# Attention's reciprocal sums: from two TensorE transposes to a store and two broadcast loads

## The chip, the cores and the metric

The kernel runs on one core of a Trainium2 chip. A core has five engines, each with its own queue of instructions, worked off in order: TensorE (PE, matrix products, transposes among them), VectorE (DVE), ScalarE (ACT), GpSimd (POOL) and SyncE (SP, which here only issues DMAs). Engines wait for each other through semaphores. A DMA is issued by an instruction on the queue of SP, ACT or POOL, and whatever stands behind that instruction waits with it. TensorE writes into PSUM, eight banks of 2 KB per partition; GpSimd works on SBUF here. The metric is the device time of one execution in microseconds (us), as the median of several runs.

## The reference, cut to what matters

The program is two layers of a diffusion trunk (a convolution layer, then an attention layer, each with a SwiGLU FFN) over 1024 latent tokens and 256 context tokens. The change touches the attention of the second layer: 16 heads of 64 channels, which share 4 key/value heads, 1280 keys.

```python
def gqa_sdpa(q, k, v):
    B, Q, H, Dh = q.shape
    qg = q.reshape(B, Q, N_KV_HEADS, KV_GROUP, Dh)
    s = jnp.einsum("bqkgd,bskd->bkgqs", qg, k).astype(jnp.float32) * (Dh ** -0.5)
    p = jax.nn.softmax(s, axis=-1).astype(v.dtype)
    o = jnp.einsum("bkgqs,bskd->bqkgd", p, v)
    return o.reshape(B, Q, H * Dh)
```

The kernel leaves the division of the softmax to the end: it multiplies the values with the bare exponentials and scales the result by the reciprocal of their sum. That last step is what is changed.

## The kernel before

Attention works in **units**. A unit is one key/value head `t` (with its four query heads) and one block `qt` of 128 queries; there are 4 x 8 = 32. Units run in two streams of 16: first the queries 0 to 511, then 512 to 1023. In each unit:

- `load_q` (L1102) fetches the queries from DRAM by a DMA on GpSimd's queue, into one of two slots. Unit n+2 uses the slot of unit n, so its load waits until TensorE has read that one.
- `scores` (L1116 to L1124): for each of the four heads, TensorE computes 128 x 1280 scores into one of two places in PSUM; VectorE scales them and takes the row minimum (L1122); ScalarE takes the exponential and sums it along the row (L1124). The sums of the four heads stand in `sums[:, 0, :]`, with the query as the partition.
- `values` (L1128 to L1158) goes over ten blocks `j` of 128 keys. TensorE transposes the four heads' exponentials (L1134); ScalarE rounds them into a high part (L1137) and VectorE takes the rest (L1138); TensorE multiplies both with the values (L1140, L1141) into the one PSUM bank of the kind `av`. The two halves of a value row (high and low part) come out on the two halves of the partitions, with the channel as the partition and the query along the row.
- the end of `values`: VectorE takes the reciprocal of the sums (L1145). GpSimd copies each of the four reciprocals 64 times along the row (L1147). ScalarE copies one half of the bank to `tmp` (L1151) and VectorE adds the other (L1152), for each half of the partitions. Two TensorE transposes (L1155) turn the copied reciprocals, so that the query runs along the row, into the same bank `av`, and VectorE multiplies (L1156). `done` stores the result in DRAM (`od`, L1450, GpSimd's queue), except for the last unit of a stream, whose result stays in SBUF as `olast`.

`values` of a unit and `scores` of the next are woven into one another (`attn_stream`), and a scheduler then sets each engine's order by priorities; the products with the values are put later by `lav`. So TensorE finishes a unit's values at about the time when it has finished the scores of the second unit after it.

What stands around it: the first units of stream one run beside the last query projections (`qkv`), the others of that stream **alone**. At the end of stream one comes the **hand-over**: `out_proj` loads `od` back (L1485), splits it into a high and a low part (L161 on ScalarE, L164 on VectorE), the last unit's from `olast`, and projects it. The second stream runs in the background of that, of the norm behind it (L761, L763) and of the FFN for the first half of the queries; `pump` gives it a share of each step. At its **end** the second `out_proj` does the same, with `T1` as its input, `T2` and `T5` as the two split parts. `T1`, `T5` and `HS` hold the exponentials before that.

Of the kernel before, what the change touches and what calls it, by code (L numbers as in the profile page):

```python
# [8 lines left out]
F32 = mybir.dt.float32  # L9
# [3 lines left out]
ALU = mybir.AluOpType  # L13
AX = mybir.AxisListType

P = 128
# [4 lines left out]
TOK = CTX + SEQ  # L21
# [3 lines left out]
NH, NKV, HD = 16, 4, 64  # L25
# [30 lines left out]
class Kern:  # L56
# [1071 lines left out]
    def values(self, t, Ps, sums, dst, done):  # L1128
        nc, c = self.nc, self.c
        av = self.bank("av")  # L1130
        for j in range(NJ):
            tp = self.bank("pt")
            for h in range(4):
                nc.tensor.transpose(tp[:, h * P:(h + 1) * P], Ps[h][:, j * P:(j + 1) * P], c["ident"])  # L1134
            ph, pl = self.ptring[self.ptslot % len(self.ptring)]
            self.ptslot += 1
            nc.scalar.copy(ph, tp)  # L1137
            nc.vector.tensor_tensor(pl, tp, ph.bitcast(F32), op=ALU.subtract)  # L1138
            with self.later(self.lav):
                nc.tensor.matmul(av, lhsT=self.value(t, j), rhs=ph, start=j == 0, stop=False)  # L1140
                nc.tensor.matmul(av, lhsT=self.value(t, j), rhs=pl, start=False, stop=j == NJ - 1)  # L1141
            yield 0.87

        r = sums[:, 1, :]
        nc.vector.reciprocal(r, sums[:, 0, :])  # L1145
        rx = self.sb(256)
        nc.gpsimd.tensor_copy(rx.rearrange("p (h d) -> p h d", d=HD), r.unsqueeze(2).to_broadcast([P, 4, HD]))  # L1147
        tmp = self.sb(256).rearrange("p (a q) -> p a q", q=P)
        v = av.rearrange("p (a b q) -> p a b q", b=2, q=P)
        for b, r, o in ((0, slice(0, 64), slice(64, 128)), (1, slice(64, 128), slice(0, 64))):  # L1150
            nc.scalar.copy(tmp[r], v[o, :, b, :])  # L1151
            nc.vector.tensor_tensor(dst[r], v[r, :, b, :], tmp[r], op=ALU.add)  # L1152
        rb = self.bank("av")
        for a in range(2):
            nc.tensor.transpose(rb[:, a * P:(a + 1) * P], rx[:, a * P:(a + 1) * P], c["ident"])  # L1155
        nc.vector.tensor_tensor(dst, dst, rb[:, 0:256].rearrange("p (a q) -> p a q", q=P), op=ALU.mult)  # L1156
        done()
        yield 0.1  # L1158

# [270 lines left out]
    def attention(self, final, qr):  # L1430
        nc, a, c = self.nc, self.a, self.c
        kbuf = self.T("T3", [P, 2 * TOK], F32R)
        pr1 = self.T("T1", [P, 3, TOK])
        prh = self.T("HS", [P, 4, TOK])
        ptt = self.T("T2", [P, 4, 2, 512], F32R)
        self.ptring = [(ptt[:, i, 0], ptt[:, i, 1]) for i in range(4)]
# [6 lines left out]
        def dst(q0):  # L1443
            def of(t, q):
                if (t, q % 4) == (NKV - 1, 3):
                    return self.olast, lambda: None
                st = self.sb(256).rearrange("p (a q) -> p a q", q=P)

                def done():
                    nc.gpsimd.dma_start(self.od[:, 2 * t:2 * t + 2, q * P:(q + 1) * P], st)  # L1450
                return st, done
            return of
# [11 lines left out]
        pr4 = None  # L1464
        for us in self.attn_stream(units, (self.kub, kbuf), dst(0), True):
            if self.bgq:
                self.pump(self.rate * us)
            elif pr4 is None:
                pr4 = self.T("T5", [P, 3, TOK])
                self.pring = self.pring[:4] + [pr4[:, 0], pr4[:, 1], pr4[:, 2]] + self.pring[4:]  # L1470
                self.set_banks(**alone)
                self.sring = [0, TOK]
# [78 lines left out]
        yacc, n = self.acc(CTX), CTX  # L1551
# [172 lines left out]
```

## Time and profile before

| | |
|---|---|
| median of 3 runs | 2939.41 us (2938.95 to 2943.35) |
| the profiled execution | 2938.98 us, its span 2937.2 us |
| TensorE clock granted, mean | 0.987 |
| attention units | first reciprocal at 1605.2 us, last at 2362.6 us |

How to read it. The span runs from the first instruction to the last. A row of a group of instructions names the line, the engine, the operation, what it writes and reads (tiles by name, `ps` is PSUM, `T` any of the large tiles `T1` to `T6`, `cst` the constants with the identity), shapes, how often, then the busy time in us and the mean of one in ns, then the idle time of the engine just before them and who ended it. PEld is TensorE's loading of weights, which runs beside its products. A chain of work is followed back from the last instruction of a window: at each step to what released it. Where a chain is all PE, other engines had nothing to do with the length of that stretch.

### The profile page before, as it was taken

How to read it: one execution, taken by the hardware profiler on the slowest of the kernel's cores; microseconds unless marked ns; L12 is line 12 of the kernel's file. 1: busy time of each engine (PE TensorE's matmuls, PEld its weight loads, DVE VectorE, ACT ScalarE, POOL GpSimd, SP SyncE). 2: the span in 40 equal slices, each digit the busy share in tenths (PEclk: the TensorE clock that was granted, in tenths of full speed). 3: DMA queues.
4: the chain of work that ended last, by engine and by line, in shares of the span. 5: the costliest groups of instructions: out<-in, count | busy, mean ns of one | idle time of the engine just before them, and what ended most of it. 6: DMA issues, size and time to landing. Idle time of an engine off the chain costs nothing.

```text
span 2937.2 us, 42731 instructions
## 1 busy us (share of the span) xinstructions
PE 2847.7 (97%) x16462; PEld 2446.1 (83%) x16462; DVE 2160.7 (74%) x3746; ACT 1335.5 (45%) x2229; POOL 222.6 (8%) x377
## 2 busy tenths in 40 slices
PE   7999989999999999999999999989999999999998
PEld 6888877888888889989888787767777778889997
DVE  6887788847556378877786899786666666786777
ACT  5222255532222245544445688645555543444444
POOL 0000001011022001000011111110000000010000
PEclk9999999999999999999999999999999999999999
DMA  6443444334356224333345211322222143353332
GB/s 249 140 120 98 116 131 145 135 116 143 115 175 198 65 74 165 114 104 112 109 156 170 88 46 46 97 87 81 66 73 83 60 149 99 110 170 104 102 98 75
DMA packets 131755, 336.58 MB, mean 115 GB/s; under 512 B 31328, under 2 KB 52864, under 8 KB 130656
## 3 DMA queue, kind: packets, MB, share of 16 engines
q1 hardware_dynamic: 78016, 222.33, 24.1%
q0 software_dynamic: 29344, 103.83, 10.7%
q10 hardware_dynamic: 24192, 7.70, 1.1%
q8 instruction: 129, 2.11, 0.3%
q14 instruction: 74, 0.61, 0.1%
HBM read 289.50 MB, written 38.93 MB: 112 GB/s over the span
## 4 chain that ended last, share of the span: by engine, by line
PE 86%; DVE 7%; ACT 2%; issue 2%; DMA 2%; ACTq 0%; POOL 0%; SPq 0%; DVEq 0%; POOLq 0%
PE ps L172 15%; PE ps L173 15%; PE ps L174 15%; PE ps L875 4%; PE ps L877 4%; PE ps L876 4%; PE ps L1116 4%; PE ps L1134 4%; PE ps L1140 2%; PE ps L454 2%; PE ps L455 2%; PE ps L456 2%; PE ps L1141 2%; PE ps L185 1%; PE ps L183 1%
## 5 line engine op out<-in xcount | busy, mean ns | idle before, releaser
L172 PE MATMUL ps<-T,wh 128*128 128x512 f32 (+1 forms) x1360 | 502.5, 370 | 1.4 <-ACT T L161 0.8
L174 PE MATMUL ps<-T,wl 128*128 128x512 f32 (+1 forms) x1360 | 500.4, 368 | 2.0 <-DVE wl L148 2.0
L173 PE MATMUL ps<-T,wh 128*128 128x512 f32 (+1 forms) x1312 | 481.4, 367 | 0.2 <-DVE T L164 0.2
L144 ACT CAST wh<-wr 128x1024 fp32r<-128x1024 f32 (+1 forms) x217 | 225.0, 1037 | 419.9 <-PE ps L173 307.2
L148 DVE TENSOR_TENSOR wl<-wr,wh 128x1024 fp32r<-128x1024 f32 (+1 forms) x217 | 261.9, 1207 | 168.5 <-ACT wh L144 167.1
L875 PE MATMUL ps<-T,wh 128*128 128x256 f32 x1092 | 310.7, 285 | 5.0 <-ACT wh L161 4.5
L876 PE MATMUL ps<-T,wh 128*128 128x256 f32 x1092 | 306.5, 281 | 0.0
L877 PE MATMUL ps<-T,wl 128*128 128x256 f32 x1092 | 305.4, 281 | 0.2 <-DVE wl L164 0.2
L1138 DVE TENSOR_TENSOR T<-ps,T 128x512 fp32r<-128x512 f32 x320 | 216.8, 687 | 107.6 <-ACT T L1137 106.8
L172 PEld LDWEIGHTS ps<-T,wh 128*128 128x128 f32 x1360 | 257.8, 190 | 43.7 <-ACT T L1506 1.7
L174 PEld LDWEIGHTS ps<-T,wl 128*128 128x128 f32 x1360 | 257.7, 190 | 42.4 <-DVE wl L148 2.2
L173 PEld LDWEIGHTS ps<-T,wh 128*128 128x128 f32 x1312 | 248.5, 189 | 38.2 <-DVE T L164 1.3
L1137 ACT CAST T<-ps 128x512 fp32r<-128x512 f32 x320 | 186.0, 586 | 191.1 <-PE ps L1134 177.6
L173 PE MATMUL ps<-HS,wh 128*128 128x512 f32 x656 | 257.9, 393 | 0.0
L172 PE MATMUL ps<-HS,wh 128*128 128x512 f32 x608 | 238.4, 392 | 0.9 <-ACT wh L144 0.9
L174 PE MATMUL ps<-HS,wl 128*128 128x512 f32 x608 | 237.5, 391 | 0.0
L875 PEld LDWEIGHTS ps<-T,wh 128*128 128x128 f32 x1092 | 206.1, 189 | 11.2 <-ACT wh L161 6.7
L876 PEld LDWEIGHTS ps<-T,wh 128*128 128x128 f32 x1092 | 206.6, 189 | 0.5
L877 PEld LDWEIGHTS ps<-T,wl 128*128 128x128 f32 x1092 | 206.2, 189 | 0.6 <-DVE wl L164 0.4
L1134 PE MATMUL ps<-cst,T 128*128 128x128 f32 x1100 | 189.6, 275 | 3.2 <-DVE T L1138 3.1
L1122 DVE TENSOR_SCALAR_CACHE_REDUCE T<-ps,rq 128x1280 f32<-128x1280 f32 x110 | 170.0, 1546 | 27.9 <-PE ps L1116 22.1
L1134 PEld LDWEIGHTS ps<-cst,T 128*128 128x128 f32 x1100 | 132.6, 141 | 49.5 <-DVE T L1138 30.8
(377 smaller groups left out, 6195.9 us busy)
## 6 DMA issues: line engine op xcount, KB each, us to landing
wr<-in_w SPq DMA_DIRECT2D x170, 512.0 KB, 3.6
wr<-in_pw SPq DMA_DIRECT2D x35, 512.0 KB, 3.5
HV<-in_wmodT POOLq DMA_DIRECT2D x56, 256.0 KB, 4.1
q<-in_wmodT POOLq DMA_DIRECT2D x56, 256.0 KB, 3.9
KB<-in_w SPq DMA_DIRECT2D x24, 512.0 KB, 3.6
HR<-in_w SPq DMA_DIRECT2D x23, 512.0 KB, 3.7
q<-in_w SPq DMA_DIRECT2D x23, 512.0 KB, 4.2
q<-qsd POOLq DMA_DIRECT2D x32, 256.0 KB, 3.3
```

What stands on the lines that cost most here:

```text
L144: nc.scalar.copy(hi, raw)
L148: nc.vector.tensor_tensor(lo, raw, hi.bitcast(F32), op=ALU.subtract)
L172: nc.tensor.matmul(out[:, :n], lhsT=wh, rhs=xh, start=k == 0, stop=False)
L173: nc.tensor.matmul(out[:, :n], lhsT=wh, rhs=xl, start=False, stop=False)
L174: nc.tensor.matmul(out[:, :n], lhsT=wl, rhs=xh, start=False, stop=k == nk - 1)
L875: nc.tensor.matmul(out, lhsT=wh, rhs=bh, start=first and k == 0, stop=False, **skip)
L876: nc.tensor.matmul(out, lhsT=wh, rhs=bl, start=False, stop=False, **skip)
L877: nc.tensor.matmul(out, lhsT=wl, rhs=bh, start=False, stop=k == 3, **skip)
L1122: nc.vector.tensor_scalar(out=pt, in0=sc, scalar1=rq[:, h:h + 1], scalar2=None, op0=ALU.mult, op1=ALU.min, accum_out=mn)
L1134: nc.tensor.transpose(tp[:, h * P:(h + 1) * P], Ps[h][:, j * P:(j + 1) * P], c["ident"])
L1137: nc.scalar.copy(ph, tp)
L1138: nc.vector.tensor_tensor(pl, tp, ph.bitcast(F32), op=ALU.subtract)
```

## The change

The reciprocal is taken at the start of `values`, and the transposes, the copies for them and VectorE's multiply are gone. In their place three DMAs on GpSimd's queue: the 128 x 4 reciprocals go to DRAM turned (`rsd`, four rows of 128 numbers, stored as 512 pieces of four bytes), and two loads bring them back into `rb`, each row repeated over 64 partitions. GpSimd then multiplies the sum of the halves by `rb`. The copies and adds of the two halves stay as they are. There are two places for `rb`, at the ends of `T1` and `T5`, used in turn (only that in `T1` until `T5` is free). `rsd` has a place of its own for each unit.

```diff
     def values(self, t, Ps, sums, dst, done):
         nc, c = self.nc, self.c
         av = self.bank("av")
+        r = sums[:, 1, :]
+        nc.vector.reciprocal(r, sums[:, 0, :])
+        rd = self.rsd[self.unit]
+        rb = self.rbs[self.unit % len(self.rbs)]
+        self.unit += 1
+        nc.gpsimd.dma_start(rd.rearrange("h q -> q h"), r)
+        rv = rd.rearrange("(a b) q -> b a q", b=2)
+        for b in range(2):
+            nc.gpsimd.dma_start(rb[b * HD:(b + 1) * HD], rv[b:b + 1].to_broadcast([HD, 2, P]))
         for j in range(NJ):
...
-        r = sums[:, 1, :]
-        nc.vector.reciprocal(r, sums[:, 0, :])
-        rx = self.sb(256)
-        nc.gpsimd.tensor_copy(rx.rearrange("p (h d) -> p h d", d=HD), r.unsqueeze(2).to_broadcast([P, 4, HD]))
         tmp = self.sb(256).rearrange("p (a q) -> p a q", q=P)
         v = av.rearrange("p (a b q) -> p a b q", b=2, q=P)
         for b, r, o in ((0, slice(0, 64), slice(64, 128)), (1, slice(64, 128), slice(0, 64))):
             nc.scalar.copy(tmp[r], v[o, :, b, :])
             nc.vector.tensor_tensor(dst[r], v[r, :, b, :], tmp[r], op=ALU.add)
-        rb = self.bank("av")
-        for a in range(2):
-            nc.tensor.transpose(rb[:, a * P:(a + 1) * P], rx[:, a * P:(a + 1) * P], c["ident"])
-        nc.vector.tensor_tensor(dst, dst, rb[:, 0:256].rearrange("p (a q) -> p a q", q=P), op=ALU.mult)
+        nc.gpsimd.tensor_tensor(dst, dst, rb, op=ALU.mult)
         done()
         yield 0.1
@@ attention
-        pr1 = self.T("T1", [P, 3, TOK])
+        def place(tag):
+            t = self.T(tag, [P, 3 * TOK + 2 * P])
+            return t[:, :3 * TOK].rearrange("p (i n) -> p i n", i=3), t[:, 3 * TOK:].rearrange("p (a q) -> p a q", q=P)
+        pr1, rb = place("T1")
+        self.rbs, self.unit = [rb], 0
+        self.rsd = self.dp.tile([2 * NKV * 4, 4, P], F32, tag="rsd", name="rsd")
...
-                pr4 = self.T("T5", [P, 3, TOK])
+                pr4, rb = place("T5")
+                self.rbs.append(rb)
```

The scheduler's order moves with it. The lines of the changed kernel are 1143 for L1134, 1149 and 1150 for L1140 and L1141, 1147 for L1138, 1157 for L1152, 1457 for L1450, 1493 for L1485 and 1508 for L1500. Three places.

TensorE while attention runs alone, around the end of a head's scores (L1116); `T_13569` and `HS` hold exponentials, `T_13571` and `T_13572` the split ones, `HV` and `HR` values. Before:

```order
L1116 MATMUL ps<-KB,q 128x512
L1116 MATMUL ps<-KB,q 128x256 x2
L1116 MATMUL ps<-KB,q 128x512
L1155 MATMUL ps<-cst,sb 128x128 x2
L1116 MATMUL ps<-KB,q 128x512 x2
L1134 MATMUL ps<-cst,HS 128x128
L1134 MATMUL ps<-cst,T_13569 128x128
L1134 MATMUL ps<-cst,HS 128x128
L1134 MATMUL ps<-cst,T_13569 128x128
L1140 MATMUL ps<-T_13571,HV 128x512
L1141 MATMUL ps<-T_13571,HV 128x512
L1140 MATMUL ps<-T_13571,HV 128x512
```

The changed kernel (`T_14072` holds exponentials too):

```order
L1116 MATMUL ps<-KB,q 128x512 x4
L1116 MATMUL ps<-KB,q 128x256 x2
L1116 MATMUL ps<-KB,q 128x512 x4
L1143 MATMUL ps<-cst,T_13569 128x128
L1143 MATMUL ps<-cst,T_14072 128x128 x3
L1143 MATMUL ps<-cst,T_13569 128x128
L1143 MATMUL ps<-cst,T_14072 128x128 x3
L1116 MATMUL ps<-KB,q 128x256 x2
L1116 MATMUL ps<-KB,q 128x512
L1149 MATMUL ps<-T_13572,HV 128x512
L1150 MATMUL ps<-T_13572,HV 128x512
L1149 MATMUL ps<-T_13572,HV 128x512
```

The pair L1155 is gone, and ten scores and eight transposes stand in one piece each where before they were cut up differently from unit to unit; this piece comes again in every unit of the alone stage, and before only in the last one and the first.

GpSimd at the hand-over, from the last `q` load before it to the loads of `x2d`. Before:

```order
L1102 DMA q<-qsd 128x4x128
L1450 DMA od<-sb 128x2x128
L1485 DMA HS<-od 128x2x512 x3
L1147 COPY sb<-sums 128x256
L1450 DMA od<-sb 128x2x128
L1485 DMA HS<-od 128x2x384
L1500 DMA HS<-x2d 128x2x512 x3
```

The changed kernel, where L1136 stores the reciprocals, L1139 loads them back and L1158 multiplies:

```order
L1102 DMA q<-qsd 128x4x128
L1158 TENSOR_TENSOR sb<-sb,T_14072 128x256
L1457 DMA od<-sb 128x2x128
L1136 DMA rsd<-sums 128x4x1
L1139 DMA T_14072<-rsd 64x2x128 x2
L1493 DMA HS<-od 128x2x512 x3
L1158 TENSOR_TENSOR sb<-sb,T_13569 128x256
L1457 DMA od<-sb 128x2x128
L1493 DMA HS<-od 128x2x384
L1508 DMA HS<-x2d 128x2x512 x2
L1158 TENSOR_TENSOR olast<-olast,T_14072 128x256
```

The last unit's store of reciprocals and its loads now stand ahead of the loads of `od`, and the multiply of the unit before it between those. In a unit of the alone stage the order is the same without the loads of `od`: store, two loads, `q` load, multiply, `od` store.

VectorE at the end of the second stream, where it splits the input of the second output projection (L164, with `T_19816` or `T_19785` as the tile that lies in `T5`). Before:

```order
L1152 TENSOR_TENSOR olast<-ps,sb 64x256
L164 TENSOR_TENSOR T_19816<-T_19810,T_19815 128x512 x2
L1152 TENSOR_TENSOR olast<-ps,sb 64x256
L164 TENSOR_TENSOR T_19816<-T_19810,T_19815 128x512
L1156 TENSOR_TENSOR olast<-olast,ps 128x256
L164 TENSOR_TENSOR T_19816<-T_19810,T_19815 128x512 x3
```

The changed kernel:

```order
L1157 TENSOR_TENSOR olast<-ps,sb 64x256
L164 TENSOR_TENSOR HS<-sm,HS 128x512
L1157 TENSOR_TENSOR olast<-ps,sb 64x256
L164 TENSOR_TENSOR T_19785<-T_19779,T_19784 128x512 x6
L164 TENSOR_TENSOR T_19785<-T_19779,T_19784 128x2x384
```

The splits stand behind the last add, and the first of them waits for GpSimd's last multiply, which reads `rb` out of `T5`.

## The prediction

> **What bounds the kernel now.** I read the page first, then the windows of the attention, then the chain of work in each of them.
>
> ```profile
> span 2937.2 us, 42731 instructions
> PE 2847.7 (97%) x16462; PEld 2446.1 (83%) x16462; DVE 2160.7 (74%) x3746; ACT 1335.5 (45%) x2229; POOL 222.6 (8%) x377
> ```
>
> TensorE (PE) is busy for 97% of the span. The change sits in attention alone, from 1573 to 2394 us, so the question is what ends last there. The windows give it by stage (us, then busy time of PE, weight loads, VectorE, ScalarE, GpSimd, each with its number of instructions, then clock and DMA).
>
> ```profile
> 1665.00:1840.00 175.00, 170.43 (x1027) 139.84 (x1025) 159.78 (x263) 142.67 (x240) 25.20 (x41) 1.00 0.19 50
> 1840.00:1880.00 40.00, 37.15 (x198) 28.86 (x198) 33.52 (x55) 29.96 (x51) 9.12 (x13) 1.00 0.42 135
> 1970.00:2365.00 395.00, 394.96 (x2029) 311.00 (x2028) 262.50 (x387) 217.36 (x338) 28.46 (x46) 1.00 0.26 76
> ```
>
> Three stages. From 1665 to 1840 attention runs **alone**: PE shows 97%, but VectorE 91%. From 1840 to 1880 is the **hand-over** to the first output projection, with PE idle 2.9 us. From 1970 to 2365 the second half of the queries runs **beside** the FFN and PE is never idle. The chain of work names the releasers (shares of the window by engine and line; L1155 is the pair of transposes that goes).
>
> ```profile
> by line: PE ps L1134 20.2%; PE ps L1116 18.0%; PE ps L1140 14.2%; PE ps L1141 13.2%; DVE T L1138 10.1%; issue 7.6%; DVE T L1122 4.4%; ACT T L1137 4.3%; DVE HS L1122 3.7%; DVE sb L1152 2.2%; PE ps L1155 1.4%; ACT sb L1151 0.5%; ACT T L1124 0
> by line: PE ps L174 17.4%; PE ps L173 17.4%; PE ps L172 17.4%; PE ps L1116 15.7%; PE ps L1134 15.0%; PE ps L1140 8.1%; PE ps L1141 7.8%; PE ps L1155 1.2%; issue 0.0%
> L1155 PE MATMUL ps<-cst,sb 128*128 128x128 f32 x28 | 5.7, 285 | 0.0
> ```
>
> Beside the FFN every step of the chain is PE, so what leaves PE is gained; alone, VectorE and ScalarE hold a quarter of it, so removing PE work need not be.
>
> **The change part by part.** There are 32 units (a key/value head times 128 queries). Each loses two PE transposes (L1155) and a VectorE multiply out of PSUM (L1156), and gets one GpSimd multiply, a store of the reciprocals and two broadcast loads. GpSimd's copy L1147 goes.
>
> *Beside the FFN.* L1155 is 1.2% of a 395 us chain, 4.7 us for the 28 matmuls (14 units), 0.34 us a unit. All of it goes. The multiply moves to an engine that waits most of the time, and VectorE has 132 us idle there, so nothing takes its place. **-4.7 us.** Below, the gain is at least the 0.22 us a unit that the pair costs alone, 3.1 us.
>
> *Alone.* The pieces of the chain (start, length, what) show how a unit runs; each starts with the last scores of a head (L1116).
>
> ```profile
> 1796.27 0.73 PE ps L1116 x3
> 1797.00 0.23 PE ps L1155 x2
> ...
> 1809.28 0.74 PE ps L1116 x3
> ...
> 1825.67 0.74 PE ps L1116 x3
> ...
> 1833.50 1.48 DVE T L1122 x2
> ...
> 1837.63 0.33 DVE sb L1152
> 1837.96 1.19 DVE T L1138 x2
> 1839.15 1.48 DVE T L1122 x2
> ...
> 1840.68 0.74 PE ps L1116 x3
> 1836.85 2.33 PE L1116 MATMUL ps<-T,q 128*128 128x512 f32 x10
> ```
>
> Before, two patterns alternate: 1796.27 to 1809.28 is 13.01 us, 1809.28 to 1825.67 is 16.39 us, so a unit takes 14.70 us. Only the last unit, 1825.67 to 1840.68, issues ten scores in one piece, as the last row (timeline) shows, and takes 15.01 us: VectorE is the chain from 1832.81 to 1840.55. The order of the changed kernel has those ten scores in every unit. So I price its unit from this one: 15.01, less 0.22 for L1155, less what L1156 is worth.
>
> ```profile
> 1841.11 0.69 DVE L1138 TENSOR_TENSOR T<-ps,T 128x512 fp32r<-128x512 f32 x1
> 1841.72 0.41 DVE L1156 TENSOR_TENSOR sb<-sb,ps 128x256 f32<-128x256 f32 x1
> 1842.05 1.55 DVE L1122 TENSOR_SCALAR_CACHE_REDUCE T<-ps,rq 128x1280 f32<-128x1280 f32 x1
> ```
>
> L1156 holds the next L1122 back by 0.33 us (1841.72 to 1842.05). The exp behind it queues on ScalarE behind casts, so I take half, 0.165. That gives 15.01 - 0.22 - 0.165 = 14.63, against 14.70: 0.07 us times 11 units, **-0.8 us**. If nothing of either is worth anything, it is +0.31 times 11 = +3.4; if both patterns stay and both savings count whole, -0.55 times 11 = -6.
>
> The added wait is on GpSimd's queue: store, two loads that wait for the store to land, the q load (L1102) for a later unit, the multiply, the store of the result. How long the store of 512 four-byte pieces takes, no row shows, so I bound it.
>
> ```profile
> q1 hardware_dynamic: 78016, 222.33, 24.1%
> q10 hardware_dynamic: 24192, 7.70, 1.1%
> od<-sb POOLq DMA_DIRECT2D x30, 128.0 KB, 2.6
> x1d<-KB POOLq DMA_DIRECT2D x8, 128.0 KB, 2.0
> T<-in_xT SPq DMA_DIRECT2D x4, 512.0 KB, 10.6
> L1102 POOL DMA_DIRECT2D q<-qsd x12 | 9.2, 770 | 79.2 <-PE ps L1116 74.1 <-PE ps L1134 5.1
> ```
>
> Each DMA engine gets 32 pieces. A packet of q10 takes 1.1% of 16 engines' 2937 us over 24192, 21 ns; one of q1, far larger, 145 ns. With the quickest store's 2.0 us as the fixed part, that is 2.7 to 6.6 us; I take 4, between od's 2.6 and that end, and keep the slowest landing of the page, 10.6, for a rival. The q load's row says that before it waited 74.1 us for PE in 12 issues. It cannot go before PE has read the slot, and this comes some 10 us after the reciprocal (scores end at 1841.4, the reciprocal is at 1845.27, a unit is 14.7); store, 4 us and two loads are over by about 7. After it, a whole unit is left until q is read. So it is hidden, and is so up to a landing of some 8 us even before that unit is counted. Ahead of the first multiply the build sets one GpSimd instruction that no row prices; it stands in the second unit, and the q load behind it is for a unit that starts 15 us later.
>
> The multiply is bounded by a one-input copy and by a blocked one (POOL rows of the timeline and of the groups):
>
> ```profile
> L1147 POOL COPY sb<-sums 128x256 f32<-128x256 f32 x14 | 6.6, 472 | 46.1 <-PE ps L1134 23.2 <-issue 18.5 <-DVE sums L1145 4.5
> 2133.91 1.36 POOL L1147 COPY sb<-sums 128x256 f32<-128x256 f32 x1
> 2133.81 1.22 DVE L148 TENSOR_TENSOR wl<-wr,wh 128x1024 fp32r<-128x1024 f32 x1
> ```
>
> It costs 0.40 (the copy without disturbance) to 1.36 us; I take 0.6, near the copy. Its reader is a store that nobody reads for long, so between the ends it costs nothing. [...] The one long copy started while VectorE ran L148, which reads two SBUF inputs. [...] In the attention alone no VectorE instruction reads two SBUF tensors, and beside the FFN VectorE is idle a third of the time. So the sum stays as it is.
>
> *Hand-over.* GpSimd, ScalarE and VectorE rows of the timeline, in order of time:
>
> ```profile
> 1845.27 0.18 DVE L1145 RECIPROCAL sums<-sums 128x4 f32<-128x4 f32 x1 [0.47 <-ACT T L1124]
> 1848.28 2.16 POOL L1485 DMA_DIRECT2D HS<-od  x3 [5.14 <-PE ps L1134]
> 1852.81 1.14 ACT L161 CAST T<-HS 128x512 fp32r<-128x512 f32 x2
> 1854.44 0.73 POOL L1450 DMA_DIRECT2D od<-sb  x1 [3.59 <-DVE sb L1156]
> 1860.72 0.83 ACT L161 CAST T<-HS 128x768 fp32r<-128x768 f32 x1 [2.05 <-DMA HS<-od]
> ```
>
> After, the last unit's store and its two loads stand ahead of the three od loads (L1485). They are issued at 1845.27 + 0.2 + 0.8 + landing + 1.1, so with 4 us at 1851.4, 3.1 us late. ScalarE's splits (L161) and the casts behind them move by as much, but ScalarE waited 2.05 us for the fourth od load, which stays at its time, because the multiply of the last but one unit is ready soon after its adds and saves L1156's time. **+1.0 us**, with bounds 0 (landing 2.7) and +3.7 (landing 6.6).
>
> *End.* GpSimd's last multiply reads the broadcast from T5, and the split of the second output projection writes T5.
>
> ```profile
> 2389.64 1.29 DVE L164 TENSOR_TENSOR T<-T,T 128x512 fp32r<-128x512 f32 x2 [0.25 <-ACT T L161]
> 2390.97 0.43 DVE L1152 TENSOR_TENSOR olast<-ps,sb 64x256 f32<-64x256 f32 x1
> 2393.00 0.50 PE L172 MATMUL ps<-T,wh 128*128 128x512 f32 x1 [0.82 <-ACT T L161]
> ```
>
> The first splits (L164), at 2389.64 before, now wait for L1152's end at about 2391 plus 0.6 of multiply and two semaphores: some 2 us late. PE waited 0.82 us at 2393.0 anyway and has other matmuls to do: **+0.7 us**, between 0 and +1.5.
>
> *The seven other units* (two at the start, three in the hand-over, two later): 0.22 to 0.34 us each, **-1.7 us**.
>
> The sum is -4.7 - 0.8 + 1.0 + 0.7 - 1.7 = -5.5 us. The profiled execution took 2938.98 us (span 2937.2); the three runs' median, 2939.41, is 0.43 above it. So 2933.5 there, and 2934 against the median, which is 0.18% less. About 0.2% (5.9 us, below 2933.5 or above 2945.3) can be told from no change, so this forecast lies at that edge.
>
> **The rivals.**
> A. *Both savings whole in the attention alone.* The unit gets 0.37 to 0.55 us shorter, not 0.07, and the hand-over costs nothing: -4.7 - 5 - 1.7 + 0.4 = -11, 2928. For it: VectorE is the chain's longest run there and loses 0.33 us a unit. Against: the one unit with the new order was the slowest of its stage.
> B. *The new order is worse.* The ten scores wait for VectorE whatever else goes: +3.4 alone, hand-over +2, 2939 to 2940, no change. For it: VectorE's run of 7.74 us in that unit has neither L1155 nor L1156 in it.
> C. *Slower: GpSimd's queue turns in the round trip through DRAM.* One mechanism, the store's landing, at the hand-over: everything behind the store (od loads, multiply, od store) moves with it. With the page's slowest landing, 10.6 us, the od loads go 9.7 us late, of which ScalarE's 2.05 are covered: +7.6 in place of +1.0, the sum is +1.1, and the time 2940.5. It eats the whole gain from a landing of 9.5 us on and shows as slower from some 15, 2946; from some 19 (8, plus a unit of 14.7, less the q load's own 3 to 4) the q loads of the alone stage are late too, in every unit. For it: no row has four-byte pieces, and every unit adds 512. Against: 32 pieces a DMA engine at the price of the largest packets give 6.6.
>
> **How the numbers follow.** The forecast, with a range of its own from 2930 to 2938, has 0.50; A 0.20, B 0.15, C 0.15. The range of 2926 to 2943 leaves out a little of A and more than half of C, together under 0.2. Faster by over 0.2% is A and somewhat under half of the forecast: 0.42. Within 0.2% is the rest of the forecast, B and the near end of C: 0.48. Slower by over 0.2% is C's far end: 0.10.
>
> **What the changed profile would show.** No L1155 and 64 fewer transposes; from 1970 on, the same instructions 4 to 5 us sooner against their start, with PE still busy throughout. Alone, heads' last scores every 14.6 us, all units alike. The store of the reciprocals landing in about 4 us, and the q loads still waiting for PE, not for a DMA. At the hand-over the od loads some 3 us later against the reciprocal. Wrong would be: q loads waited for by PE's L1116, a unit over 14.8 us alone, PE idle beside the FFN, or a first multiply that takes GpSimd far longer than 0.6 us.

## The result and the profile after

The changed kernel took 2944.86 us in the median of 18 runs, against 2939.42 us before in as many: a ratio of 1.0018, with a 95% interval of 1.0010 to 1.0025. It is slower by 0.18%. The forecast was 2934, and the range ended at 2943. The profiled execution has 6.8 us more span (the page's first lines, as shown of before):

```profile
span 2944.0 us, 42628 instructions
PE 2847.0 (97%) x16398; PEld 2447.9 (83%) x16398; DVE 2150.5 (73%) x3714; ACT 1336.4 (45%) x2229; POOL 296.2 (10%) x473
```

TensorE does a little less work in a longer span. The windows of the same three stages (columns as ahead of the prediction) say where it now waits.

```profile
1665.00:1840.00 175.00, 168.24 (x1003) 137.73 (x1001) 155.55 (x250) 144.05 (x239) 52.48 (x76) 1.00 0.28 59
1840.00:1880.00 40.00, 30.80 (x158) 23.94 (x159) 26.35 (x44) 22.66 (x40) 14.19 (x20) 0.91 0.41 125
1970.00:2365.00 395.00, 393.91 (x2015) 311.22 (x2014) 262.29 (x377) 217.74 (x339) 57.70 (x85) 1.00 0.37 79
```

The first and the last stage look as before. The hand-over does not: TensorE is busy for 30.8 us of 40, before 37.15, and the granted clock is 0.91. To place the loss I follow the reciprocals of the units (timeline of VectorE, L1132, before L1145; units counted from 0). Those of units 15, 17, 18 and 31, after, and of 17, 18 and 31 before (unit 15's, at 1845.27, stands ahead):

```profile
1844.64 0.18 DVE L1132 RECIPROCAL sums<-sums 128x4 f32<-128x4 f32 x1 [0.33 <-ACT T L1124]
...
1927.52 0.16 DVE L1132 RECIPROCAL sums<-sums 128x4 f32<-128x4 f32 x1
...
1989.01 0.17 DVE L1132 RECIPROCAL sums<-sums 128x4 f32<-128x4 f32 x1
...
2369.55 0.18 DVE L1132 RECIPROCAL sums<-sums 128x4 f32<-128x4 f32 x1 [1.19 <-ACT T L1124]
```

```profile
1919.50 0.16 DVE L1145 RECIPROCAL sums<-sums 128x4 f32<-128x4 f32 x1
...
1979.36 0.17 DVE L1145 RECIPROCAL sums<-sums 128x4 f32<-128x4 f32 x1
...
2362.58 0.18 DVE L1145 RECIPROCAL sums<-sums 128x4 f32<-128x4 f32 x1 [1.20 <-ACT T L1124]
```

| Stretch, us | before | after | difference | forecast |
|---|---|---|---|---|
| start to unit 0 | 1605.19 | 1604.54 | -0.65 | 0 |
| unit 0 to 3 | 64.18 | 64.29 | +0.11 | -0.5 |
| unit 3 to 15, attention alone | 175.90 | 175.81 | -0.09 | -0.8 |
| unit 15 to 18, hand-over and first projection | 134.09 | 144.37 | +10.28 | -0.2 |
| unit 18 to 31, beside the FFN | 383.22 | 380.54 | -2.68 | -4.4 |
| unit 31 to the end of the span | 574.62 | 574.45 | -0.17 | +0.4 |
| sum | 2937.20 | 2944.00 | +6.80 | -5.5 |

The forecast's column is the prediction's terms laid on these stretches, with 0.2 to 0.34 us for each single unit that falls into them. One stretch holds the whole loss. Its first 8.65 us are there by unit 17 (82.88 against 74.23). GpSimd, ScalarE and TensorE in it, from the timeline of the changed kernel (start, length, what, in brackets the idle time ahead and what ended it):

```profile
1845.12 0.77 POOL L1136 DMA_DIRECT2D rsd<-sums  x1 [0.92 <-DVE sums L1132]
1853.58 1.21 POOL L1139 DMA_DIRECT2D T<-rsd  x2 [7.69 <-DMA rsd<-sums]
1854.77 2.19 POOL L1493 DMA_DIRECT2D HS<-od  x3
1860.55 1.14 ACT L161 CAST T<-HS 128x512 fp32r<-128x512 f32 x2 [8.04 <-DMA HS<-od]
1862.95 1.12 PE L1143 MATMUL ps<-cst,T 128*128 128x128 f32 x4 [7.87 <-DVE T L1147]
```

GpSimd issues the store of the last unit's reciprocals at 1845.12 and can issue the two broadcast loads only at 1853.58, when the store has landed. The od loads go behind them, at 1854.77: 10.1 us after the reciprocal, before 3.0 (1845.27 to 1848.28). ScalarE has the splits of od (L161) in its order ahead of the casts that TensorE needs, and stands still for 8.04 us; TensorE runs dry for 7.87. And it does not come back at full speed (windows of the changed kernel):

```profile
1850.00:1855.00 5.00, 4.74 (x28) 3.27 (x27) 2.98 (x6) 2.03 (x5) 1.42 (x3) 1.00 0.05 3
1855.00:1860.00 5.00, 0.08 (x1) 0.00 (x0) 0.00 (x0) 0.00 (x0) 3.44 (x5) 0.92 0.67 168
1860.00:1863.00 3.00, 0.05 (x1) 0.05 (x1) 1.49 (x3) 2.45 (x5) 0.00 (x0) 0.50 0.86 332
1863.00:1865.00 2.00, 2.00 (x7) 1.75 (x8) 1.96 (x4) 2.00 (x5) 0.72 (x1) 0.50 0.02 4
1865.00:1867.00 2.00, 2.00 (x11) 1.67 (x10) 1.21 (x3) 0.81 (x2) 0.00 (x0) 0.75 0.72 194
1867.00:1869.00 2.00, 1.93 (x12) 1.26 (x11) 2.00 (x4) 1.33 (x3) 0.00 (x0) 1.00 0.01 2
```

The clock column falls to 0.50 during the idle time and is back at 1.00 only after some 3 us of work (TensorE works from 1862.95; the clock is 0.52 from 1865.5 to 1866 and 1.00 behind that); between 1862.95 and 1867 TensorE loses about 1.5 us to that (2.0 us at 0.50, 2.0 at 0.75).

The row of 1850 to 1855 has one more thing: while the store is under way, the DMA engines show almost nothing, 0.05 of their time and 3 GB/s. No other data packet is in the trace's records then: those of the store itself are over by 1846.9, and the 0.05 is one 16 KB instruction fetch, which takes 3.7 us (1.1 in the median from 1500 to 2400). The experiments start there.

### The profile page after: what moved, and what is told of

Its sections match the earlier page's. It is cut to its first block, busy times and chain, and to the rows that moved or that the text cites. A ratio compares the mean times of both kernels' runs of the same rounds, so it can differ in the third digit from the quotient of the medians.

```text
span 2944.0 us, 42628 instructions
## 1 busy us (share of the span) xinstructions
PE 2847.0 (97%) x16398; PEld 2447.9 (83%) x16398; DVE 2150.5 (73%) x3714; ACT 1336.4 (45%) x2229; POOL 296.2 (10%) x473
## 3 DMA queue, kind: packets, MB, share of 16 engines
q0 software_dynamic: 32416, 108.10, 11.7%
## 4 chain that ended last, share of the span: by engine, by line
PE 84%; DVE 9%; ACT 3%; issue 2%; DMA 2%; ACTq 0%; SPq 0%; DVEq 0%; POOL 0%
PE ps L172 15%; PE ps L173 15%; PE ps L174 15%; PE ps L875 4%; PE ps L877 4%; PE ps L876 4%; PE ps L1116 4%; PE ps L1143 4%; PE ps L1149 2%; PE ps L454 2%; PE ps L455 2%; PE ps L456 2%; PE ps L1150 2%; PE ps L185 1%; PE ps L184 1%
## 5 line engine op out<-in xcount | busy, mean ns | idle before, releaser
L875 PEld LDWEIGHTS ps<-T,wh 128*128 128x128 f32 x1092 | 206.1, 189 | 11.5 <-ACT wh L161 6.9
```

Source lines behind the costliest of these rows:

```text
L875: nc.tensor.matmul(out, lhsT=wh, rhs=bh, start=first and k == 0, stop=False, **skip)
```

## The experiments

All are edits of the changed kernel. "The step to 17" is the time from unit 15's reciprocal to unit 17's: 74.23 us before, 82.88 after.

### Whose queue: the broadcast loads of one unit moved to SyncE

The first theory was that of the prediction's rival C: GpSimd's queue waits for the store, and the od loads stand behind it. The rival: the small pieces slow down the transfers themselves.

```diff
+        eng = nc.sync if self.unit == 16 else nc.gpsimd
         for b in range(2):
-            nc.gpsimd.dma_start(rb[b * HD:(b + 1) * HD], rv[b:b + 1].to_broadcast([HD, 2, P]))
+            eng.dma_start(rb[b * HD:(b + 1) * HD], rv[b:b + 1].to_broadcast([HD, 2, P]))
```

(the counter is one ahead at this place, so 16 is unit 15)

> The changed kernel with one thing else: the two broadcast loads of the last unit before the first output projection are issued by SyncE, whose queue is empty there, and not by GpSimd; every other instruction of GpSimd and all of TensorE's stand in the same order. Theory Q (GpSimd's queue: it waits 7.7 us for the store of the reciprocals to land, with the od loads behind it, and TensorE runs dry for 7.9 us): the od loads are issued at or before 3 us after the last reciprocal (changed kernel: 10.1 us, before: 3.0), the step from that unit's reciprocal to the next one falls from 37.97 to 28 to 30 us, TensorE has no idle piece over 2 us there, and the time falls by 8 to 10 us to 2935 to 2937. Rival D (the 512 small pieces and the broadcasts slow down every transfer, the od loads among them; what stands behind what in GpSimd's queue is not the point): the od loads are issued earlier but land late, the step stays over 34 us and the time over 2941.

Measured: 2943.57 us, ratio 1.0012 (1.0003 to 1.0021); the step to 16 37.46 us, to 17 82.41. GpSimd and ScalarE (timeline; lines are one higher than in the changed kernel), then the DMA issues of 1844 to 1868 with their size and median time to landing:

```profile
1847.73 0.77 POOL L1136 DMA_DIRECT2D rsd<-sums  x1 [1.20 <-DVE sums L1132]
1850.46 2.15 POOL L1494 DMA_DIRECT2D HS<-od  x3 [1.96 <-ACT T L1147]
1861.26 1.14 ACT L161 CAST T<-HS 128x512 fp32r<-128x512 f32 x2 [6.16 <-DMA HS<-od]
```

```profile
HS<-od POOLq DMA_DIRECT2D x3, 512.0 KB, 11.4
T<-rsd SPq DMA_DIRECT2D x2, 64.0 KB, 8.3
rsd<-sums POOLq DMA_DIRECT2D x1, 2.0 KB, 9.2
```

The od loads are issued on time, 3.2 us after the reciprocal, and hardly anything is won: they land 11.4 us after their issue. In the kernel before it was 5.3 (its DMA issues, 1840 to 1866):

```profile
HS<-od POOLq DMA_DIRECT2D x3, 512.0 KB, 5.3
```

**The queue alone is not the cause.** Waiting in GpSimd's queue was only one of two ways to be late, and without it the other costs nearly as much.

### How many pieces: 128 and 256 in place of 512

```diff
-        nc.gpsimd.dma_start(rd.rearrange("h q -> q h"), r)
+        nc.gpsimd.dma_start(rd.rearrange("h q -> (h q)").rearrange("(q h) -> q h", h=4), r)
```

```diff
-        nc.gpsimd.dma_start(rd.rearrange("h q -> q h"), r)
+        nc.gpsimd.dma_start(rd.rearrange("h q -> (h q)").rearrange("(a q b) -> q a b", a=2, b=2), r.rearrange("q (a b) -> q a b", a=2))
```

> The changed kernel with the store of the reciprocals in 128 pieces of 16 bytes (as they lie in SBUF) in place of 512 of 4 bytes, so the layout in DRAM is another and each query is scaled by a wrong sum; all instructions stand in the same order on every engine. If the landing is a price per piece (8.2 us for 512, of which 2.0 fixed, so 12 ns a piece): landing 3.5 us, the od loads at the hand-over 4 to 5 us sooner, the step over it 32 to 34 us, the time 2939 to 2941. If the landing is the round trip to DRAM and does not depend on the pieces: landing 8 us as before, the step 38, the time 2944 to 2946.

> The changed kernel with the store of the reciprocals in 256 pieces of 8 bytes, so the layout in DRAM is another and each query is scaled by a wrong sum; all instructions stand in the same order. With a price per piece and DMA engine, from the two landings measured at the hand-over (8.2 us for 512 pieces of 4 bytes, 2.0 for 128 of 16: 6.2 us for 24 pieces more on each of 16 engines, 0.26 us a piece): landing 4.1 us, weight loads beside the FFN 3.6 to 4.2 us in the median, the step from unit 15 to 17 some 78 us (82.9 and 76.4 with the other two), the time 2938 to 2941. If a piece under some size costs a step of its own and not its share: landing 8 us or 2 us.

Both ran with every instruction of the changed kernel in its place; the reciprocals lie in another order in DRAM, so only the time is read. With 128 pieces: 2935.83 us, ratio 0.9988 (0.9979 to 0.9997), step to 17 76.44. With 256: 2937.96 us, 0.9994 (0.9984 to 1.0004), step 76.63. Both are faster than had been expected. The DMA issues beside the FFN (1990 to 2355), of before, of the changed kernel, with 256 and with 128 pieces:

```profile
wr<-in_w SPq DMA_DIRECT2D x33, 512.0 KB, 3.6
od<-sb POOLq DMA_DIRECT2D x12, 128.0 KB, 2.6
```

```profile
wr<-in_w SPq DMA_DIRECT2D x34, 512.0 KB, 4.7
od<-sb POOLq DMA_DIRECT2D x13, 128.0 KB, 9.0
rsd<-sums POOLq DMA_DIRECT2D x13, 2.0 KB, 10.2
```

```profile
wr<-in_w SPq DMA_DIRECT2D x34, 512.0 KB, 3.6
rsd<-sums POOLq DMA_DIRECT2D x12, 2.0 KB, 3.5
```

```profile
wr<-in_w SPq DMA_DIRECT2D x33, 512.0 KB, 3.6
rsd<-sums POOLq DMA_DIRECT2D x12, 2.0 KB, 2.0
```

The same 2 KB land in 10.2, 3.5 and 2.0 us: it is the pieces, not the round trip. At the hand-over it is 8.2, 3.0 and 1.7. The price is not one number per piece, as the second expectation had it (4.1): spread over 16 engines, the step from 256 to 512 pieces costs 0.33 us a piece and engine (8.2 less 3.0, over 16), that from 128 to 256 0.16 (3.0 less 1.7, over 8). The runs change the number of the pieces and their size together, so which of the two makes the last step so dear stays open. The rows show something else too: while 512 pieces go out, the weight loads (wr), which SyncE issues on a queue of their own, land later too (4.7 us for 3.6), and od's stores over three times as late (9.0 for 2.6).

### Which queue: od loads, or store and loads, on SyncE

```diff
-                nc.gpsimd.dma_start(o[:, 2 * q:2 * q + 2, :n], self.od[:, 2 * q:2 * q + 2, q0:q0 + n])
+                (nc.gpsimd if q0 else nc.sync).dma_start(o[:, 2 * q:2 * q + 2, :n], self.od[:, 2 * q:2 * q + 2, q0:q0 + n])
```

```diff
+        eng = nc.sync if self.unit == 16 else nc.gpsimd
-        nc.gpsimd.dma_start(rd.rearrange("h q -> q h"), r)
+        eng.dma_start(rd.rearrange("h q -> q h"), r)
```

(the second also with the loads by `eng`, as above)

> The changed kernel with the od loads of the first output projection issued by SyncE in place of GpSimd, the store staying on GpSimd's queue. Theory E: the first three od loads are issued some 2 to 4 us after the reciprocal and land only when the store has landed, 8 to 11 us after their issue; the step from unit 15 to 17 is 80 to 84 us, the time 2942 to 2946. Rival S: they land 4 to 5 us after their issue, and the step falls by 3 us or more (the fourth, behind a store that stands in GpSimd's queue, stays late), the time is below 2942.

> The changed kernel with the store and the two broadcast loads of unit 15 issued by SyncE, on the hardware queue, and nothing of unit 15's on GpSimd's queue ahead of the od loads; all else in the same order. Theory E: the store holds the DMA engines from this queue too, the od loads land 8 to 11 us after their issue (with SyncE issuing only the loads: 11.4), the step from unit 15 to 17 is 80 to 83 us, the time 2942 to 2945. Rival S (only GpSimd's software queue is slow with small pieces): od loads land in 4 to 6 us, the step is 74 to 77 us, the time 2935 to 2938.

Measured: 2942.59 us, 1.0011 (1.0002 to 1.0020), step to 17 83.29; and 2943.32 us, 1.0010 (1.0001 to 1.0019), step 81.69, both as theory E had it. (In the first, ScalarE's and TensorE's order at the hand-over moved a little.) The DMA issues of 1844 to 1868 of the two:

```profile
HS<-od SPq DMA_DIRECT2D x3, 512.0 KB, 11.9
rsd<-sums POOLq DMA_DIRECT2D x1, 2.0 KB, 9.2
```

```profile
HS<-od POOLq DMA_DIRECT2D x3, 512.0 KB, 10.5
rsd<-sums SPq DMA_DIRECT2D x1, 2.0 KB, 8.6
```

With the store on one queue and the od loads on the other, either way round, the od loads land 10.5 to 11.9 us after their issue. The broadcast loads aren't what delays them: with 128 pieces they stand at the same place, and the od loads land in 5.4 us. **The store holds up the transfers of either queue.** A single case from the changed kernel, beside the FFN: the weight load that SyncE issues at 2058.06, with a store of 2055.18 under way, is the only one of its window (2056 to 2065). Its issue, and SyncE's DMA queue in that window (packets, MB, share of the 16 engines' time):

```profile
wr<-in_w SPq DMA_DIRECT2D x1, 512.0 KB, 10.8
q1 hardware_dynamic: 46, 0.19, 57.0%
```

So the records do not show idle engines once another transfer is there: 46 packets hold the engines for 57% of 9 us, some 1.8 us each. The same queue from 1990 to 2355, before and after:

```profile
q1 hardware_dynamic: 4752, 17.30, 15.2%
```

```profile
q1 hardware_dynamic: 4784, 17.39, 25.3%
```

The packets are as many and as large, and take 0.31 us each in place of 0.19. With 256 pieces the share is 16.7%. Whether the pieces are held in the engines or on the way to DRAM behind them, no run here shows.

### The store twice

```diff
         nc.gpsimd.dma_start(rd.rearrange("h q -> q h"), r)
+        nc.gpsimd.dma_start(rd.rearrange("h q -> q h"), r)
```

> The changed kernel with the store of the reciprocals issued twice in each unit, the loads waiting for both. Theory E: the two hold the DMA engines one after the other, landing 14 to 17 us; a unit of the attention alone becomes longer than 14.76 us, 16 to 19, because the q loads stand behind them on GpSimd's queue, and weight loads issued beside the FFN land in 6 to 10 us in the median (changed kernel 4.7, before 3.6); the time is 2960 to 3000. Rival F (the landing is a fixed round trip that two stores share): landing 9 to 10, units of 14.8, the time 2944 to 2949.

Measured in a single run: 3063.14 us, units of 22 us in the attention alone, weight loads beside the FFN 7.1 us in the median (2106 to 2487, its units 18 to 31). GpSimd in one such unit (timeline), and the DMA queue of GpSimd on both pages, changed kernel first (packets, MB, share of the engines):

```profile
1788.38 0.78 POOL L1137 DMA_DIRECT2D rsd<-sums  x1 [9.99 <-DMA rsd<-sums]
1797.31 1.20 POOL L1140 DMA_DIRECT2D T<-rsd  x2 [8.14 <-DMA rsd<-sums]
1798.50 0.79 POOL L1102 DMA_DIRECT2D q<-qsd  x1
...
1801.08 0.77 POOL L1136 DMA_DIRECT2D rsd<-sums  x1
```

```profile
q0 software_dynamic: 32416, 108.10, 11.7%
```

```profile
q0 software_dynamic: 33440, 108.16, 11.7%
```

The direction held, and the weight loads lie within the 6 to 10 us expected; the unit and the time do not (16 to 19 us and 2960 to 3000): the second store waits on GpSimd for the first, 9.99 us, the loads wait 8.14 for the second, and with the issues that is more than the 14.76 us of a unit, so GpSimd's queue becomes the bound. That is rival C's mechanism; here it decides in every unit, in the changed kernel it does not. The 32 stores more are 1024 packets more, 32 each. In the packet records of the changed kernel a store is 16 packets of 128 bytes and 16 of four; those of the store of 2055.18 are over by 2056.9, and it lands 11.3 us after its issue. A wait behind those packets does not explain the weight load's 10.8 us: its own begin at 2059.04, after the store's, and one of them takes 7.7 us itself.

### One unit scaled as before; two; sixteen and one

In the first kernel unit 15, in the second 15 and 31, in the third 0 to 15 and 31 keep transposes and VectorE's multiply:

```diff
+        old = self.unit == 15
...
+        if old:
+            pb = self.bank("av")
+            for a in range(2):
+                nc.tensor.transpose(pb[:, a * P:(a + 1) * P], rx[:, a * P:(a + 1) * P], c["ident"])
+            nc.vector.tensor_tensor(dst, dst, pb[:, 0:256].rearrange("p (a q) -> p a q", q=P), op=ALU.mult)
+        else:
+            nc.gpsimd.tensor_tensor(dst, dst, rb, op=ALU.mult)
```

(with the reciprocal and GpSimd's copy at their old place; the second kernel has 15 and 31, the third 0 to 15 and 31 in the first line)

> The changed kernel, but the one unit before the first output projection (unit 15) scaled as before, with transposes and VectorE's multiply, so that no store of small pieces is pending there. Theory E (the 16 DMA engines are held by a store of 512 four-byte pieces for some 8 us, whatever queue a transfer comes from; at this one place TensorE runs dry for it): od loads issued some 3 us after the last reciprocal and landing 4 to 5 us after that, the step from unit 15's reciprocal to unit 17's falls from 82.9 to 74 to 76 us (before: 74.2), the time is 2935 to 2938. Rival O (the new order of TensorE's work at the hand-over is what costs, with any landing): the step stays over 80 us and the time over 2942.

> The changed kernel with the two units that stand right before an output projection (15 and 31) scaled as before, all others by the change. If the hand-over is the only place where the store's 8 us are not covered: the saving beside the FFN (2.8 us) stays, the hand-over costs nothing, and without a store pending at the second output projection TensorE loses its 0.9 us of idle time there: 2935.5 to 2937 against 2939.5 of before, and 0 to 1 us below the kernel with unit 15 alone done so. If the store before the second projection is hidden anyway: the same as that one, 2936 to 2938.

> The kernel before for units 0 to 15 and the last one (transposes and VectorE's multiply), the change in units 16 to 30 only, beside the FFN. Theory Q, with the hand-over as the only loss: up to the first output projection as before, beside the FFN the pair of transposes gives 0.21 us a unit, 2.7 to 3.2 us in all, and the time is 2936 to 2937. Rival P (the forecast's price of the pair, 0.34 us a unit): 2934 to 2935. Rival G (GpSimd's multiply and the small pieces cost beside the FFN what the transposes gave): 2939 to 2940.

Measured: 2937.10 us, ratio 0.9988 (0.9980 to 0.9997); 2938.99 us, 0.9994 (0.9985 to 1.0003); 2936.39 us, 0.9989 (0.9980 to 0.9998). On the chip of the second one the changed kernel was run once more:

> The changed kernel itself, on the same chip as the one with units 15 and 31 done as before: 2943 to 2946, 7 to 9 us above that one.

It took 2944.47 us, 1.0016 (1.0007 to 1.0025), 5.5 us above the second kernel, less than expected. The second kernel itself lies above either time that was expected of it: what the old scaling of unit 31 would give can't be seen. The first one's hand-over (timeline of GpSimd, and the DMA issues of 1844 to 1868):

```profile
1846.36 2.18 POOL L1506 DMA_DIRECT2D HS<-od  x3 [3.94 <-PE ps L1145]
```

```profile
HS<-od POOLq DMA_DIRECT2D x3, 512.0 KB, 4.9
```

Without a store under way the od loads land in 4.9 us, and some eight of the lost microseconds (144.37 less 136.29, unit 15 to 18) come back from one unit of 32. The step to 17 was expected at 74 to 76 us and is 83.75, since unit 17 stands elsewhere in that kernel's order; to unit 18 it is 134.09 before. The kernels with 128 and 256 pieces have the changed kernel's order and give back over 6 of the 8.65 us. So the order of the work (rival O) isn't what costs most; of the last 2 us that isn't shown. The three kernels can't be told apart by their intervals. Two of them are faster than the kernel before, by 0.11 to 0.12%: that is what the change gives where no such store stands at the hand-over.

### Two dead transposes a unit

```diff
+        junk = self.bank("av")
+        for a in range(2):
+            nc.tensor.transpose(junk[:, a * P:(a + 1) * P], c["ident"], c["ident"])
         nc.gpsimd.tensor_tensor(dst, dst, rb, op=ALU.mult)
```

> The changed kernel with the two transposes per unit kept as dead work (the identity into the bank that is free then, read by nobody); the scheduler orders the engines anew, so it is read by stage. Alone, if TensorE is not what bounds a unit: units of 14.76 us as in the changed kernel, within 0.05. If TensorE bounds it: 14.95 to 15.0. If the order decides, units of two lengths again, as before the change. Beside the FFN 2.7 to 3.2 us longer than the changed kernel for the same instructions.

Measured in a single run: 2944.36 us. Alone, the units are 14.4 to 14.8 us, but for one of 19.69 and three of 11.5 to 13.5; from unit 3 to 15 it takes 175.37 us, no longer than without the pair (175.81) or before (175.90). So the pair costs nothing that can be seen there. Beside the FFN, unit 18 to 31 is 380.34 us, not longer than the changed kernel's 380.54, against the expectation; but unit 31 stands elsewhere in this order, and from unit 18 to the end of the span it is 956.97, against 954.99, and 957.84 before. In that longer stretch TensorE is busy for 942.9 us before, 939.6 in the changed kernel and 942.9 with the dead pair: 3.3 us for 14 pairs, 0.24 each. So the pair's price is there, and two of the 2.85 us gained go with it; the order was made anew, and it is one run.

## Why the prediction was wrong

**The step that failed is the hand-over: "+1.0 us, with bounds 0 (landing 2.7) and +3.7 (landing 6.6)".** It measured +8.65 us to unit 17. By its own working a landing of 8.2 us would have given +5.2. Three things in it were off.

1. *The landing.* It was taken as 4 us and bounded at 6.6, with the price of the largest packets for each of 32 pieces on an engine. It is 8.2 there. A packet's row tells nothing of the price of a four-byte piece: 0.33 us by the runs with 256 and 512 pieces, over twice the 145 ns that the prediction took for the largest packets. By those with 128 and 256 it is 0.16; what makes the step to four bytes so dear, no run here shows.
2. *What waits for it.* Prediction and rival C let the od loads wait in GpSimd's queue. That wait is real in the trace (7.69 us), but taking it away gave 0.5 us of the step, and the od loads landed late from either queue (10.5 to 11.9 us after their issue). What the store does to the other transfers is enough by itself.
3. *What it costs.* The prediction covered lateness with ScalarE's 2.05 us, since the fourth od load "stays at its time", and counted the rest as such. The fourth went 19.2 us after the reciprocal (GpSimd's L1493 at 1863.85), before 11.7, so nothing was covered. And ScalarE's order puts od's splits ahead of the casts that feed TensorE, so TensorE ran dry for 7.87 us and then worked at a granted clock of 0.50.

Between 17 and 18 there are 1.63 us more (61.49 against 59.86). The kernel with units 0 to 15 as before shows the same there, with no store at the hand-over (windows of before and of that kernel, unit 17 to 18):

```profile
1919.50:1979.36 59.86, 49.83 (x231) 37.97 (x231) 52.34 (x104) 27.89 (x43) 6.25 (x11) 0.89 0.25 79
```

```profile
1919.02:1980.58 61.56, 51.70 (x230) 39.60 (x229) 52.06 (x103) 27.84 (x43) 8.60 (x14) 0.86 0.26 80
```

Its mean clock is 0.86 in place of 0.89: after a gap of 5.51 us, which both kernels have, it comes back some 2 us later. Of the kernels with the new path and this order, those with 128 and 256 pieces and the one with the loads on SyncE have 59.8 to 60.1 us there; the other two of the hand-over and the second profile of the changed kernel have 61.5. What decides between the two isn't shown, and this part is not laid to the change.

With a short store some loss stays: the step to 17 is 76.44 with 128 pieces, 2.2 us above before. There the fourth od load goes 13.50 us after the reciprocal, before 11.72: the od store ahead of it is issued as soon as before (9.18 and 9.17 us), but GpSimd waits 3.57 us for its landing in place of 1.83. Whether that is all of it was not tried.

**Beside the FFN** the sign was right and the size not: -2.68 us for 13 units, 0.21 a unit, where the chain's share had given 0.34. That is about the lower bound named there, 0.22, the time of the pair where it stands alone, and the dead pair's 0.24 agrees. Why the chain gave more isn't shown. All nine kernels with the new path there have 380.2 to 380.9 us.

**Alone**, -0.09 in place of -0.8: the units came out equal, as said, but at 14.76 us each and not 14.63, and over the whole stretch as long as the two old patterns. Against the one old unit of that order, 15.01, it is 0.25 us where the prediction took 0.385 off. With the dead pair the stretch is no longer, so TensorE's pair was hardly on the path; VectorE's multiply was not tried.

**The end**, +0.7 for the projection's splits, less one unit: this execution has -0.17 from unit 31 on, and the nine kernels have 572.3 to 574.5 us there, before 574.62. A cost can't be seen; the forecast was on the high side.

**The rivals.** A fell with the stage alone. B had the stage alone without gain, but its +3.4 did not come, and it had the hand-over at +2. C named the place, the store and the price, +7.6 for a landing of 10.6 us, but as the smaller case, and its mechanism is not the whole: with GpSimd's queue free for the od loads the loss stays. That the q loads and the multiply would be hidden was right; the multiply took 0.75 us, 0.6 had been said as an estimate from the copy's 0.40, and the od stores waited for it, and once a split of the second projection (L164), for 0.9 us.

## What to carry to other kernels

A store's landing goes by its pieces here (8.2, 3.0 and 1.7 us with 512, 256 and 128 at the hand-over), and what it holds up is not its reader alone but the loads of other queues in that time (the od loads on SyncE's queue landed in 11.9 us, those of before in 5.3). Before a transposing store of four-byte pieces goes into a loop, look for the places in the kernel where a load is issued just behind it and TensorE has nothing else: 31 stores cost nothing measurable here (175.88 and 380.50 us with 128 pieces, 175.81 and 380.54 with 512, alone and beside the FFN), and one cost some 6 to 8 us. And a lateness that is covered "but for a few microseconds" can cost more than those: here TensorE ran dry for 7.87 us, came back at a granted clock of 0.50, and lost about 1.5 us more to that.

## What was not expected of the hardware

- While a 2 KB store of 512 pieces is under way alone, the records show the DMA engines nearly idle (0.05 of their time from 1850 to 1855). Idle in the records isn't free: the weight load issued at 2058.06, with such a store under way, took 10.8 us for 512 KB, which land in 3.6 in the median before, and the records show its queue's packets for 57% of the engines' time from 2056 to 2065.
- Landing of the same 2 KB, by piece: 4 bytes 8.2 us, 8 bytes 3.0, 16 bytes 1.7 at the hand-over; 10.2, 3.5 and 2.0 in the median beside the FFN.
- It made no difference whether GpSimd's or SyncE's queue issued the small pieces: 9.2 and 8.6 us.
